# First loads of a batched matmul recut: b's first tile in halves over two queues, one b tile on another queue, an early table load, and a late store in halves

## The chip, the core and the metric

The kernel runs on one core of a Trainium2 chip. The metric is device time in microseconds (us), lower is better. All outputs are right.

## The reference

```python
a = randn(1024, 64, 64)   # fp32
b = randn(1024, 64, 64)   # fp32
out = np.matmul(a, b)     # fp32, 1024 products of 64x64 by 64x64
```

16.78 MB of a and of b are read and 16.78 MB are written.

## The kernel before

a comes in 8 tiles of 128 batches (GpSimd's queue, cast to bf16 in flight), b in 16 tiles of 64 batches (SyncE's and ScalarE's queues, fp32), the output leaves in 16 tiles (GpSimd's queue). Per tile of a: VectorE regroups it, TensorE transposes, ScalarE copies the transposes out of PSUM (the memory in which TensorE's results land in this kernel). Per tile t: VectorE spreads the transposed a into a block-diagonal tile, ScalarE casts b, TensorE multiplies, ScalarE evicts the first half of the product from PSUM and VectorE the second. The parts concerned, with cuts marked:

```python
b_v = b.rearrange("(t g h) (kp u) n -> t (h kp) g (u n)", h=4, g=16, u=2)

def load_b(t):
    b_sb = b_pool.tile([128, 16, 128], fp32, name="b_sb")      # 4 buffers
    queue = nc.scalar if t in (1, 3, 5, 7) else nc.sync
    load = queue.dma_start(out=b_sb[:], in_=b_v[t])
    # ... tiles 0 and 1 wait for the second load of a's first tile
def regroup(s):
    # ...
    nc.vector.tensor_copy(a_bf[:], a_sb[:].rearrange("p h v k -> p v h k"))
def cast(t):
    # ...
    nc.scalar.copy(b_bf[:], b_sb[:])      # last tile: in four, ScalarE and VectorE in turn
def multiply(t):
    # ... products; half 0 evicted by ScalarE, half 1 by VectorE
    held[t] = [lambda: put(0, 8)]         # last tile: four pieces of 2

# main loop, in program order
for t in range(n_t):
    # spread(t+1); cast(t+1); load_b(t+4)
    # on even t: regroup(t//2 + 2), load_a(t//2 + 4)
    # multiply(t); transpose of the a tile ahead; store(t-1)
```

Of the kernel before, what the change touches and what calls it, by code (L numbers as in the profile page):

```python
# [8 lines left out]
fp32 = mybir.dt.float32  # L9
# [4 lines left out]
def kernel(  # L14
# [14 lines left out]
    nc = tc.nc  # L29
# [4 lines left out]
    n_t, n_s = B // 64, B // 128  # L34
# [6 lines left out]
    b_v = b.rearrange("(t g h) (kp u) n -> t (h kp) g (u n)", h=4, g=16, u=2)  # L41
    o_v = out.rearrange("(t gh x) (mo w) n -> t (x mo) gh (w n)", gh=8, x=8, w=4)

    consts = ctx.enter_context(tc.tile_pool(name="consts", bufs=1))
# [12 lines left out]
        consts.tile([128, 2, 16, 2, 4, 16], fp32, name=f"at_bd{i}") for i in range(N_BD)  # L57
    ]
    identity = consts.tile([128, 128], fp32)
    a_tiles, b_tiles, abf_tiles, at_tiles, bbf_tiles = {}, {}, {}, {}, {}  # L60
    held, first_a = {}, []

    def load_a(s):
        a_sb = a_pool.tile([128, 4, 16, 64], bf16, name="a_sb")
        for h in range(4):
            load = nc.gpsimd.dma_start(  # L66
                out=a_sb[:, h, :, :].rearrange("p v k -> p (v k)"), in_=a_v[s, h]
            )
            if s == 0:
                first_a.append(load)  # L70
        a_tiles[s] = a_sb

    def load_b(t):
        b_sb = b_pool.tile([128, 16, 128], fp32, name="b_sb")
        queue = nc.scalar if t in (1, 3, 5, 7) else nc.sync
        load = queue.dma_start(out=b_sb[:], in_=b_v[t])  # L76
        if t < 2:
            tc.add_manual_dep(
                load.ins,
                first_a[1].ins.name,  # L80
                mybir.DependencyInfo(
                    mybir.DependencyClass.Sync, mybir.DependencyReason.DATA
                ),
                reason="first tile of a goes ahead",
            )
        b_tiles[t] = b_sb

    def regroup(s):
        a_sb = a_tiles.pop(s)
        a_bf = work.tile([128, 16, 4, 64], bf16, name="a_bf")  # L90
        nc.vector.tensor_copy(a_bf[:], a_sb[:].rearrange("p h v k -> p v h k"))  # L91
        abf_tiles[s] = a_bf
        at_tiles[s] = work.tile([128, 2, 32, 2, 4, 4], fp32, name="at_sb")

    def transpose(s, j):
        a_cols = abf_tiles[s][:].rearrange("p v h k -> p v (h k)").bitcast(fp32)
        for wl in range(2):
            at_ps = t_psum.tile([128, 4, 128], fp32, name="at_ps")
            for vo in range(4):
                nc.tensor.transpose(  # L100
                    at_ps[:, vo, :], a_cols[:, 4 * vo + 2 * j + wl, :], identity[:]
                )
            nc.scalar.copy(  # L103
                at_tiles[s][:, j, :, wl, :, :],
                at_ps[:].rearrange("p vo (g mp) -> p g mp vo", mp=4),
            )

    def spread(t):
        half = slice(16 * (t % 2), 16 * (t % 2) + 16)
        bd = bd_tiles[t % N_BD]  # L110
        for h in range(4):
            rows = slice(32 * h, 32 * h + 32)
            nc.vector.tensor_copy(  # L113
                bd[rows, :, :, :, h, :].rearrange("p j g wl mo -> p j (g wl) mo"),
                at_tiles[t // 2][rows, :, half, :, :, :].rearrange(
                    "p j g wl mp vo -> p j (g wl) (mp vo)"
                ),
            )

    def cast(t):  # L120
        b_bf = work.tile([128, 16, 128], bf16, name="b_bf")
        b_sb = b_tiles.pop(t)
        if t < n_t - 1:
            nc.scalar.copy(b_bf[:], b_sb[:])  # L124
        else:
            for gq in range(4):
                rows = slice(4 * gq, 4 * gq + 4)
                if gq % 2:
                    nc.vector.tensor_copy(b_bf[:, rows, :], b_sb[:, rows, :])  # L129
                else:  # L130
                    nc.scalar.copy(b_bf[:, rows, :], b_sb[:, rows, :])  # L131
        bbf_tiles[t] = b_bf

    def store(t):
        for piece in held.pop(t):
            piece()

    def multiply(t):
        at_bd = bd_tiles[t % N_BD][:].rearrange("p j g wl h mo -> p j g (wl h mo)")
        at_bd = at_bd.bitcast(bf16).rearrange("p j g (c u) -> p j g c u", u=2)  # L140
        b_bf = bbf_tiles.pop(t)
        last = t == n_t - 1
        o_sb = o_pool.tile([128, 8, 2, 2, 64], fp32, name="o_sb")

        def put(lo, n):
            nc.gpsimd.dma_start(  # L146
                out=o_v[t, :, lo : lo + n, :],
                in_=o_sb[:, lo : lo + n].rearrange("p gh j wl n -> p (gh j wl n)"),
            )

        def evacuate(o_ps, gh, n, copy):

            for par in range(2):
                for wl in range(2):
                    src = o_ps[64 * wl : 64 * wl + 64, :, par, :, :]
                    dst = o_sb[64 * par : 64 * par + 64, gh : gh + n, :, wl, :]
                    copy(dst, src)  # L157

        for half in range(2):
            if not last:  # L160
                o_ps = o_psum.tile([128, 4, 2, 2, 64], fp32, name="o_ps")
            for g8 in range(8):
                if last and g8 % 4 == 0:
                    o_ps = t_psum.tile([128, 2, 2, 2, 64], fp32, name="at_ps")
                g = 8 * half + g8
                gl = (g8 % 4 if last else g8) // 2
                for j in range(2):
                    for u in range(2):
                        nc.tensor.matmul(  # L169
                            o_ps[:, gl, g % 2, j, :],  # L170
                            at_bd[:, j, g, :, u],
                            b_bf[:, g, 64 * u : 64 * u + 64],
                            start=(u == 0),
                            stop=(u == 1),
                        )
                if last and g8 % 4 == 3:
                    copy = nc.scalar.copy if g8 == 3 else nc.vector.tensor_copy
                    evacuate(o_ps, g // 4 * 2, 2, copy)
            if not last:
                copy = nc.vector.tensor_copy if half else nc.scalar.copy  # L180
                evacuate(o_ps, 4 * half, 4, copy)
        if last:
            held[t] = [lambda q=q: put(2 * q, 2) for q in range(4)]
        else:
            held[t] = [lambda: put(0, 8)]

    with tc.manual_schedule():
        load_a(0)
        for t in range(B_AHEAD):
            load_b(t)  # L190
        nc.vector.memset(bd_tiles[0][:], 0.0)  # L191
        make_identity(nc, identity)
        for s in range(1, A_AHEAD):
            load_a(s)
        nc.gpsimd.memset(bd_tiles[1][:], 0.0)  # L195
        regroup(0)
        transpose(0, 0)
        transpose(0, 1)
        spread(0)
        cast(0)  # L200
        regroup(1)
        load_a(A_AHEAD)
        transpose(1, 0)
        for t in range(n_t):
            s, half = t // 2, t % 2
            if t + 1 < n_t:
                spread(t + 1)
                cast(t + 1)
            if t + B_AHEAD < n_t:
                load_b(t + B_AHEAD)  # L210
            if half == 0:
                if s + 2 < n_s:
                    regroup(s + 2)
                if s + 1 + A_AHEAD < n_s:
                    load_a(s + 1 + A_AHEAD)
            multiply(t)
            if half == 0 and s + 1 < n_s:
                transpose(s + 1, 1)
            if half == 1 and s + 2 < n_s:
                transpose(s + 2, 0)  # L220
            if t >= HOLD - 1:
                store(t - HOLD + 1)
        for t in range(n_t - HOLD + 1, n_t):
            store(t)
# [30 lines left out]
```

## Time and profile before

| | before |
|---|---|
| time, median of the first three runs | 136.94 us (136.76 to 137.51) |
| span of the profiled run | 134.8 us |
| VectorE busy | 105.0 us (78%); 90% or more in 26 of the 29 slices from 30.3 to 128.1 us |
| DMA engines busy | 90% or more in the slices from 3.4 to 121.3 us |
| b's tiles 0, 1, 2, 3 landed at | 22.7, 22.9, 33.2, 33.5 us |
| VectorE's spread(2) began at | 32.17 us |
| VectorE's last eviction ended at | 127.9 us |

The prediction shows the lines for the whole run and the tail. More of them count in what follows: the page's row of VectorE's busy tenths in 40 slices of 3.37 us, its count of DMA packets (a packet is one entry of the trace's DMA records), its list of issues for b (columns: tensor, queue, number, KB as the trace encodes the load, us to landing), and the moments of cast(1), of GpSimd's first store and of VectorE's spread(2).

```profile
DVE  5512099069999999997999999997599999999900
DMA packets 17469, 42.12 MB, mean 312 GB/s; under 512 B 1073, under 2 KB 1073, under 8 KB 17457
b_sb<-in_b_dram SPq DMA_DIRECT2D x12, 0.5 KB, 18.3
b_sb<-in_b_dram ACTq DMA_DIRECT2D x4, 0.5 KB, 16.0
```

```profile
25.48 1.91 ACT L124 CAST b_bf<-b_sb 128x2048 bf16<-128x2048 f32 x1
32.73 1.32 POOL L146 DMA_DIRECT2D out_dram<-o_sb  x1 [3.29 <-DVE o_sb L157]
32.17 3.22 DVE L113 COPY at_bd<-at_sb 32x1024 f32<-32x1024 f32 x4
```

There are 1073 packets under 512 bytes and the same 1073 under 2 KB: nothing but semaphore writes and the like lies below 2048 bytes. "0.5 KB" looks odd for a load of 1 MB; it means that the shape is not in the DMA instruction but in a shape register set just ahead of it (the trace has one MOVE_SHAPE per load).

### The profile page before, as it was taken

To read this page: it belongs to the slowest core of one execution; us is meant where nothing else is said; L and a number is where in the kernel's file an instruction comes from. 1 tells how busy PE (TensorE), PEld (TensorE's weight loads), DVE (VectorE), ACT (ScalarE), POOL (GpSimd) and SP (SyncE) were. 2 spreads that over 40 slices of the span, in tenths; PEclk is the share of its full clock that TensorE was granted. 3 is DMA by queue (a packet is one entry of the trace's DMA records).
4 is the path that set the end of the run, shared out by engine and by line. 5 is a ranking of instruction groups with operands and counts; after the bars stand their busy time and mean duration, and the time that the engine had idled before them with its cause. 6 is when DMAs were issued, how large, how long until landed. Compare 5 with 4: busy or idle time off the path is not lost.

```text
span 134.8 us, 2815 instructions
## 1 busy us (share of the span) xinstructions
PE 69.3 (51%) x1152; PEld 65.2 (48%) x1152; DVE 105.0 (78%) x143; ACT 84.5 (63%) x122; POOL 46.6 (35%) x58
## 2 busy tenths in 40 slices
PE   0007305695169709389637861956039735669000
PEld 0007205695069609289637861956039625558000
DVE  5512099069999999997999999997599999999900
ACT  0010902992998995958996896699347996637100
POOL 6949723132413350152322243323021114040820
PEclk9999999999955995955995599599955995555555
DMA  2999999999999999999999999999999999998593
GB/s 19 185 204 261 309 305 301 309 308 279 272 294 311 312 394 346 303 275 361 393 360 273 272 381 396 340 267 288 393 394 396 393 399 395 407 406 350 191 320 136
DMA packets 17469, 42.12 MB, mean 312 GB/s; under 512 B 1073, under 2 KB 1073, under 8 KB 17457
## 3 DMA queue, kind: packets, MB, share of 16 engines
q0 software_dynamic: 9008, 25.17, 66.1%
q1 hardware_dynamic: 6336, 12.58, 26.0%
q10 hardware_dynamic: 2112, 4.19, 8.1%
q8 instruction: 9, 0.15, 0.4%
q14 instruction: 4, 0.02, 0.0%
HBM read 33.55 MB, written 16.78 MB: 373 GB/s over the span
## 4 chain that ended last, share of the span: by engine, by line
DMA 65%; DVE 18%; issue 9%; POOL 3%; POOLq 1%; DVEq 0%
DMA a_sb<-in_a_dram 48%; DMA out_dram<-o_sb 16%; DVE o_sb L157 10%; DVE at_bd L113 8%; POOL out_dram L146 2%; POOL a_sb L66 1%; POOLq L250 1%; DVE a_bf L91 0%; DVEq L91 0%; POOLq L146 0%; DVEq L113 0%; POOLq L239 0%
## 5 line engine op out<-in xcount | busy, mean ns | idle before, releaser
L169 PEld LDWEIGHTS <-at_bd 128*128 128x128 bf16 x1024 | 45.8, 117 | 41.4 <-DVE o_sb L157 30.7
L169 PE MATMUL o_ps<-b_bf,at_bd 128*128 128x64 bf16 x960 | 44.7, 219 | 36.6 <-DVE o_sb L157 28.7
L113 DVE COPY at_bd<-at_sb 32x1024 f32<-32x1024 f32 x64 | 46.4, 725 | 7.9 <-ACT at_sb L103 5.9
L157 DVE COPY o_sb<-o_ps 64x512 f32<-64x512 f32 x60 | 41.3, 688 | 1.8 <-PE o_ps L169 0.8
L157 ACT COPY o_sb<-o_ps 64x512 f32<-64x512 f32 x60 | 34.8, 580 | 9.5 <-DMA out_dram<-o_sb 5.3
L146 POOL DMA_DIRECT2D out_dram<-o_sb x19 | 21.0, 1107 | 46.9 <-DVE o_sb L157 20.1
L124 ACT CAST b_bf<-b_sb 128x2048 bf16<-128x2048 f32 x15 | 28.6, 1905 | 8.7 <-DMA b_sb<-in_b_dram 8.5
L66 POOL DMA_DIRECT2D a_sb<-in_a_dram x32 | 21.5, 681 | 35.2 <-DMA a_sb<-in_a_dram 21.0
L100 PE MATMUL at_ps<-identity,a_bf 128*128 128x128 f32 x128 | 24.4, 357 | 17.3 <-DVE a_bf L91 17.3
L100 PEld LDWEIGHTS at_ps<-identity,a_bf 128*128 128x128 f32 x128 | 20.5, 190 | 17.7 <-issue 17.7
L103 ACT COPY at_sb<-at_ps 128x512 f32<-128x512 f32 x32 | 17.6, 589 | 4.8 <-PE at_ps L100 4.5
L91 DVE COPY a_bf<-a_sb 128x4096 bf16<-128x4096 bf16 x8 | 9.8, 1228 | 11.5 <-DMA a_sb<-in_a_dram 11.3
L76 ACT MOVE_SHAPE b_sb<-in_b_dram x4 | 0.7, 172 | 7.9 <-DMA a_sb<-in_a_dram 7.0
L157 ACT COPY o_sb<-at_ps 64x256 f32<-64x256 f32 x8 | 2.9, 367 | 3.0 <-PE at_ps L169 2.9
L191 DVE MEMSET at_bd<- 128x4096 f32 x1 | 3.5, 3472 | 1.7 <-PEq L239 1.7
L103 ACT ACT_TABLE_LOAD x1 | 1.3, 1283 | 4.8 <-issue 4.8
L169 PE MATMUL at_ps<-b_bf,at_bd 128*128 128x64 bf16 x64 | 3.6, 241 | 1.2 <-DVE at_bd L113 1.2
L195 POOL MEMSET at_bd<- 128x4096 f32 x1 | 3.5, 3530 | 0.0
L157 DVE COPY o_sb<-at_ps 64x256 f32<-64x256 f32 x8 | 3.4, 421 | 0.1
L131 ACT CAST b_bf<-b_sb 128x512 bf16<-128x512 f32 x2 | 1.1, 615 | 1.9 <-DMA b_sb<-in_b_dram 1.9
L129 DVE CAST b_bf<-b_sb 128x512 bf16<-128x512 f32 x2 | 0.8, 424 | 0.0
masks.py:199 POOL TENSOR_SCALAR_AFFINE_SELECT identity<-identity 128x128 f32<-128x128 f32 x1 | 0.3, 287 | 0.1
(5 smaller groups left out, 0.6 us busy)
## 6 DMA issues: line engine op xcount, KB each, us to landing
out_dram<-o_sb POOLq DMA_DIRECT2D x15, 1024.0 KB, 21.8
a_sb<-in_a_dram POOLq DMA_DIRECT2D x32, 256.0 KB, 19.8
out_dram<-o_sb POOLq DMA_DIRECT2D x4, 256.0 KB, 5.3
b_sb<-in_b_dram SPq DMA_DIRECT2D x12, 0.5 KB, 18.3
b_sb<-in_b_dram ACTq DMA_DIRECT2D x4, 0.5 KB, 16.0
```

The source lines that it names most:

```text
L66: load = nc.gpsimd.dma_start(out=a_sb[:, h, :, :].rearrange("p v k -> p (v k)"), in_=a_v[s, h])
L91: nc.vector.tensor_copy(a_bf[:], a_sb[:].rearrange("p h v k -> p v h k"))
L100: nc.tensor.transpose(at_ps[:, vo, :], a_cols[:, 4 * vo + 2 * j + wl, :], identity[:])
L103: nc.scalar.copy(at_tiles[s][:, j, :, wl, :, :], at_ps[:].rearrange("p vo (g mp) -> p g mp vo", mp=4),)
L113: nc.vector.tensor_copy(bd[rows, :, :, :, h, :].rearrange("p j g wl mo -> p j (g wl) mo"), at_tiles[t // 2][rows, :, half, :, :, :].rearrange(
L124: nc.scalar.copy(b_bf[:], b_sb[:])
L146: nc.gpsimd.dma_start(out=o_v[t, :, lo : lo + n, :], in_=o_sb[:, lo : lo + n].rearrange("p gh j wl n -> p (gh j wl n)"),)
L157: copy(dst, src)
L169: nc.tensor.matmul(o_ps[:, gl, g % 2, j, :], at_bd[:, j, g, :, u], b_bf[:, g, 64 * u : 64 * u + 64], start=(u == 0), stop=(u == 1),)
L191: nc.vector.memset(bd_tiles[0][:], 0.0)
L195: nc.gpsimd.memset(bd_tiles[1][:], 0.0)
L250: with _tile.TileContext(nc) as tc:
```

## The change

The intent: shorten the head (b's first tile sooner, transposes sooner, no table load in the way) and the tail (half of tile 14's store sooner).

```diff
+    warm = consts.tile([128, 2], fp32)
...
-        queue = nc.scalar if t in (1, 3, 5, 7) else nc.sync
-        load = queue.dma_start(out=b_sb[:], in_=b_v[t])
+        if t == 0:
+            parts = [(nc.sync, 0, 8), (nc.scalar, 8, 16)]
+        else:
+            parts = [(nc.scalar if t in (1, 5, 7) else nc.sync, 0, 16)]
+        for queue, lo, hi in parts:
+            load = queue.dma_start(out=b_sb[:, lo:hi, :], in_=b_v[t][:, lo:hi, :])
...
-        nc.vector.tensor_copy(a_bf[:], a_sb[:].rearrange("p h v k -> p v h k"))
+        for lo, hi in [(0, 1), (1, 2), (2, 3), (3, 4)] if s == 0 else [(0, 4)]:
+            # ... one copy per quarter
...
-            nc.scalar.copy(b_bf[:], b_sb[:])
+            for lo, hi in [(0, 8), (8, 16)] if t == 0 else [(0, 16)]:
+                nc.scalar.copy(b_bf[:, lo:hi, :], b_sb[:, lo:hi, :])
...
-            held[t] = [lambda: put(0, 8)]
+            whole = t < n_t - 2
+            held[t] = [lambda q=q: put(q, 8 if whole else 4) for q in ([0] if whole else [0, 4])]
...
         load_a(0)
+        nc.vector.memset(warm[:, 0:1], 0.0)
+        nc.scalar.copy(warm[:, 1:2], warm[:, 0:1])
```

More of the change, by code (lines that the diff above doesn't have):

```diff
@@ L74, in load_b @@
         b_sb = b_pool.tile([128, 16, 128], fp32, name="b_sb")
-        queue = nc.scalar if t in (1, 3, 5, 7) else nc.sync
-        load = queue.dma_start(out=b_sb[:], in_=b_v[t])
-        if t < 2:
-            tc.add_manual_dep(
-                load.ins,
-                first_a[1].ins.name,
-                mybir.DependencyInfo(
-                    mybir.DependencyClass.Sync, mybir.DependencyReason.DATA
-                ),
-                reason="first tile of a goes ahead",
-            )
+        if t == 0:
[4 more added lines that the diff above has]
+            load = queue.dma_start(out=b_sb[:, lo:hi, :], in_=b_v[t][:, lo:hi, :])
+            if t < 2:
+                tc.add_manual_dep(
+                    load.ins,
+                    first_a[1].ins.name,
+                    mybir.DependencyInfo(
+                        mybir.DependencyClass.Sync, mybir.DependencyReason.DATA
+                    ),
+                    reason="first tile of a goes ahead",
+                )
         b_tiles[t] = b_sb
@@ L90, in regroup @@
         a_bf = work.tile([128, 16, 4, 64], bf16, name="a_bf")
-        nc.vector.tensor_copy(a_bf[:], a_sb[:].rearrange("p h v k -> p v h k"))
+        for lo, hi in [(0, 1), (1, 2), (2, 3), (3, 4)] if s == 0 else [(0, 4)]:
+            nc.vector.tensor_copy(
+                a_bf[:, :, lo:hi, :],
+                a_sb[:, lo:hi, :, :].rearrange("p h v k -> p v h k"),
+            )
         abf_tiles[s] = a_bf
```

## The prediction

> **What bounds the kernel now.** I read the page's slices first, then stretches of the run, then the packet records of the DMA queues, and only then the engines' timelines. The slices' last two rows:
>
> ```profile
> DMA  2999999999999999999999999999999999998593
> GB/s 19 185 204 261 309 305 301 309 308 279 272 294 311 312 394 346 303 275 361 393 360 273 272 381 396 340 267 288 393 394 396 393 399 395 407 406 350 191 320 136
> ```
>
> The 16 DMA engines are at 90% or more from the second slice to the 37th (3.4 to 124.7 us); no compute engine is. The GB/s row looks uneven, but it counts bytes written, and `a` is read as fp32 and written as bf16. Counting a's bytes as read (twice what is written), I summed the packet records in 1 us bins: 395 to 421 GB/s in nearly every bin from 5 to 43 us, 389 to 405 in 4 us bins up to 124. So the transfers are at one rate, near 400, whatever their mix. All there is to move is 3 x 16.78 MB = 50.3 MB, which is 126 us of a 134.8 us span. What is not saturated is the first 3.4 us and the tail. The stretches of the tail (columns: PE, PEld, DVE, ACT, POOL busy, clock, DMA share, GB/s):
>
> ```profile
> 96.00:123.00 27.00, 16.11 (x281) 15.10 (x282) 26.15 (x37) 17.10 (x27) 5.22 (x4) 0.66 1.03 399
> 124.00:125.00 1.00, 0.45 (x9) 0.28 (x6) 0.96 (x3) 0.97 (x3) 0.04 (x1) 0.50 0.53 201
> 125.00:126.00 1.00, 0.00 (x0) 0.00 (x0) 0.97 (x3) 0.13 (x1) 1.00 (x2) 0.50 0.10 29
> 126.00:127.00 1.00, 0.00 (x0) 0.00 (x0) 0.96 (x3) 0.00 (x0) 1.00 (x2) 0.50 0.59 209
> 127.00:133.00 6.00, 0.00 (x0) 0.00 (x0) 0.91 (x3) 0.00 (x0) 1.69 (x3) 0.50 0.96 317
> ```
>
> The reader sees a hole: 399 GB/s up to 123, then 201, 29, 209, and only 317 afterwards. At 124 us, 2.35 MB of the output were still to go; at 400 GB/s that is 5.9 us, ending at 129.9 and not at 133.0 where the last packet ended. The tail loses 3.1 us. GpSimd and VectorE show why:
>
> ```profile
> 118.22 1.36 POOL L146 DMA_DIRECT2D out_dram<-o_sb  x1 [4.58 <-DVE o_sb L157]
> 124.97 3.00 POOL L146 DMA_DIRECT2D out_dram<-o_sb  x4 [5.38 <-issue]
> 128.23 0.72 POOL L146 DMA_DIRECT2D out_dram<-o_sb  x1 [0.26 <-DVE o_sb L157]
> ...
> 95.80 1.23 DVE L91 COPY a_bf<-a_sb 128x4096 bf16<-128x4096 bf16 x1 [2.33 <-DMA a_sb<-in_a_dram]
> 121.63 2.79 DVE L157 COPY o_sb<-o_ps 64x512 f32<-64x512 f32 x4
> 124.45 3.48 DVE L157 COPY o_sb<-at_ps 64x256 f32<-64x256 f32 x8
> ```
>
> Tile 13's store is issued at 118.22, tile 14's not before VectorE has evicted its second half at 124.42. From 95.8 us, when the last tile of a (a7) has landed at 95.7, VectorE runs without a gap to 127.9. So two clocks set the end: the landing of a7 plus 32 us of VectorE, and the drained DMA queue. The chain of waits agrees: it is DMA until 95.7, VectorE to the end of its evictions, then the last store.
>
> **What the Trainium skill says.** "DMA: Bandwidth & Descriptors", section "Issuing engines are not separate DMA queues": DMAs from ScalarE, SyncE and GpSimd run on the same 16 engines and interleave, and issuing from several saves issue time alone. This trace agrees in total (near 400 GB/s with one, two or three queues active) but the split depends on how many are active. Section "Queues, rings and completion order" says that each DMA engine goes round-robin between rows, by packet. Here: with both b queues active a gets about 195 GB/s and each b queue 104 (12 to 31 us); with SyncE's alone a gets about 255 and b 140 (33 to 37 us). Section "Anatomy of one DMA — SWDGE (gpsimd) path" puts some 2 us of fixed cost on a transfer; here 1.5 us pass from the issue at 124.97 to data at 126.5. "ScalarE: Activation LUTs", "What ACT_TABLE_LOAD costs", gives 1283 ns; the trace's one load took 1283 ns.
>
> **The change part by part.**
>
> *Head, engines.* ScalarE before:
>
> ```profile
> 8.56 4.77 ACTq L76 DMA_DIRECT2D b_sb<-in_b_dram  x1
> 13.37 1.28 ACT L103 ACT_TABLE_LOAD   x1 [4.83 <-issue]
> 14.66 2.05 ACT L103 COPY at_sb<-at_ps 128x512 f32<-128x512 f32 x4
> 22.72 1.90 ACT L124 CAST b_bf<-b_sb 128x2048 bf16<-128x2048 f32 x1 [6.01 <-DMA b_sb<-in_b_dram]
> ```
>
> The early table takes 1.28 us from in front of the copies. The regroup in four pieces (same 1.23 us of work, by estimate 0.3 us each) leaves only the last behind the fourth landing at 9.5, so the transposes start some 0.9 us earlier. The halves of b0 go at 104 GB/s on each of two queues: 0.524 MB take 5.0 us rather than 1.05 MB taking 10, so b0 lands near 17.5 instead of 22.7. The first product starts near 18.5 to 19, some 6 us earlier. But the next step on VectorE, evicting tile 0's second half, stands behind regroup(2) in program order, and that waits for a2's landing at 28.0. A2's bytes were all moved before 27 us, while both b queues were still active, and that stays so. Worth at the end: 0. No gain of the head's engines reaches the queue, which is full anyway.
>
> *Head, later casts.* With b0 on both queues b1 and b2 come behind: 1.57 MB on each at 104.5 GB/s from 11.4 is 26.5, plus 1.3 to land (as b0 had) gives 27.8; before, b1 landed at 22.9 and b2 at 33.2. So cast(1) moves from 25.5 to 27.8, then an eviction (2.4), two copies (1.1) and cast(2) near 33.1, as before (33.27). It costs VectorE perhaps 1 us near 33, hidden under the DMA.
>
> *Fourth b tile to SyncE.* ScalarE's queue now carries 3.67 MB and not 4.19. It is empty from about 26.5 rather than 31.5 until b5 goes out (issue 33.3, data 37.7, unchanged). For 5 us a gets 60 GB/s more: 0.3 MB. The same bytes of b come later. GpSimd's queue runs 0.3 MB ahead from then on; at its 257 GB/s that brings a7 in 1.2 us earlier, 94.5, and with it VectorE's run and all later stores. B's last tile comes 0.33/0.14 = 2.4 us later, 117.5 instead of 115.1. ScalarE casts then at 117.5, VectorE needs its own part near 119.5: it fits, barely.
>
> *Tile 14 in halves.* Its first half was evicted by ScalarE at 119.2. Half a store, 0.524 MB, can be issued near 119.6, right after tile 13's, and be moved in the hole from 123.7. The tail behind it is shorter by 0.524 MB at 330 GB/s (its rate after 126.5): 1.6 us. One issue is added, some 0.7 us on an idle GpSimd.
>
> Sum: 1.6 us from the store, up to 1.2 us from a7; I count the second at 0.7 of its size, 0.8. 136.94 - 2.4 = 134.5.
>
> **The rivals.**
> 1. *Only the tail counts.* A7 lands at 95.7 as before, since b5 or later tiles take the bandwidth back. For it: buffers of b free earlier at the head. Then 136.94 - 1.6 = 135.3.
> 2. *The whole hole closes.* With a7 earlier and the half store in the hole, the queue never runs empty, packets stay at 165 ns (they took 190 ns after 126.5) and the rate stays at 400: last packet 129.9, 3.1 us gained, 133.8. Against it: VectorE's last eviction and the last issue with its 1.5 us cannot come before some 128.2.
> 3. *B becomes the late one.* The final b tiles come 2.4 us later, b15 was already waited for (1.9 us before ScalarE's cast at 115.2), and a late cast(14) or cast(15) stalls products and VectorE. That would eat the 0.8 and more: 135.5 to 137.
> 4. *The head's 6 us reach the end.* Against it: no free DMA time between 4 and 123 us to take them up.
>
> **Range and chances.** The middle of 1 to 3 is 134.5; 133.4 to 136.2 covers the full hole and most of rival 3. The 2% line lies at 134.2, just below my middle: faster 0.40, same 0.57, slower 0.03.
>
> **What would show it.** B0's first cast near 17.5 and first product before 20, yet regroup(2) still near 28. B1 landing near 27.8. A7's regroup at 94 to 95. A store of half size issued near 119 and no stretch under 250 GB/s between 123 and 128. VectorE's last eviction near 126.7. Wrong would be: a7 over 2 us earlier, VectorE idle after a7, or a DMA rate well off 400 in the middle.

## More of the kernel before

On VectorE, regroup(2) stands before the eviction of tile 0, and spread(2) after it. On ScalarE, cast(1) stands before the eviction of tile 0, which stands before the copies that spread(2) needs.

## The result, and the profile after

| | before | after |
|---|---|---|
| time, median of four runs | 136.85 us | 141.65 us (141.43 to 141.96) |
| ratio | | 1.034, 95% interval 1.030 to 1.039 |
| span of the profiled run | 134.8 us | 139.1 us |
| VectorE's spread(2) | 32.17 us | 40.48 us |
| VectorE's last eviction ended | 127.9 us | 134.1 us |
| from there to the end of the span | 6.9 us | 5.0 us |

The change made the kernel slower. A ratio is the mean time of one kernel's fast runs over that of the other's of the same rounds, so it is not quite the ratio of the medians. (The median of before is given with the runs of the same chip each time.)

The page of the changed kernel, the same rows as shown of before:

```profile
GB/s 18 190 194 230 231 234 252 304 307 293 272 296 298 392 326 273 293 393 390 369 273 267 382 398 328 269 297 402 393 392 397 395 396 391 397 270 244 211 319 135
DMA packets 19036, 42.12 MB, mean 303 GB/s; under 512 B 1104, under 2 KB 3152, under 8 KB 19024
b_sb<-in_b_dram SPq DMA_DIRECT2D x1, 512.0 KB, 17.4
b_sb<-in_b_dram ACTq DMA_DIRECT2D x1, 512.0 KB, 18.4
b_sb<-in_b_dram SPq DMA_DIRECT2D x12, 0.5 KB, 21.1
b_sb<-in_b_dram ACTq DMA_DIRECT2D x3, 0.5 KB, 15.9
```

There are now 3152 - 1104 = 2048 packets between 512 bytes and 2 KB. The two halves make exactly 1024 each: 0.524 MB / 1024 = 512 bytes a packet. All other b tiles still move in packets of 2048 bytes. The halves are also listed differently (512.0 KB and not 0.5 KB: an immediate shape, no shape register). In the slices from 10 to 24 us the GB/s row is down (230 to 252, before 261 to 309): it counts written bytes, and more of what moves there is now a.

The packet records say how the engines were shared from 12 to 22 us:

| 12 to 22 us | a | b on SyncE | b on ScalarE |
|---|---|---|---|
| before: packets per us | 46.7 | 51.1 | 51.3 |
| before: GB/s (a as read) | 191 | 105 | 105 |
| after: packets per us | 73.0 | 82.1 | 81.8 |
| after: GB/s (a as read) | 299 | 42 | 42 |

In both kernels the queues move nearly equal numbers of packets, whatever the size of these (the counts show this, not how long one turn is). With packets of a quarter of the size and 1.6 times as many of them, each b queue fell from 105 to 42 GB/s, and a rose. B0's halves landed at 24.1 and 25.1 us, later than the whole tile before (22.7), and b1 and b2, which stand behind them on ScalarE's and SyncE's queues, at 35.2 and 34.8.

The engines after, ScalarE, then GpSimd, then VectorE (columns: start, us, engine, line, operation, tiles, count, and in brackets the idle time before it and what ended it):

```profile
24.13 1.99 ACT L135 CAST b_bf<-b_sb 128x1024 bf16<-128x1024 f32 x2 [9.23 <-DMA b_sb<-in_b_dram]
...
35.19 1.90 ACT L135 CAST b_bf<-b_sb 128x2048 bf16<-128x2048 f32 x1 [8.09 <-DMA b_sb<-in_b_dram]
37.00 1.75 ACT L168 COPY o_sb<-o_ps 64x512 f32<-64x512 f32 x3
...
39.64 0.92 POOL L157 DMA_DIRECT2D out_dram<-o_sb  x1 [14.73 <-ACT o_sb L168]
...
28.67 2.79 DVE L168 COPY o_sb<-o_ps 64x512 f32<-64x512 f32 x4 [3.88 <-PE o_ps L180]
40.48 2.83 DVE L123 COPY at_bd<-at_sb 32x1024 f32<-32x1024 f32 x4 [9.01 <-ACT at_sb L113]
```

Cast(1) waits 8.09 us for b1. Behind it in ScalarE's order stands the eviction of tile 0's first half, so GpSimd waits 14.73 us for its first store, and behind that the copies for spread(2), so VectorE stands idle for 9.01 us. From 40.48 us on VectorE has one gap over 0.15 us, of 0.24 us, up to the end of its last eviction at 134.08: it is the bound for the rest of the run. Before, it had waits of 0.82 and 2.33 us in that stretch, so about 2.9 of the 8.3 us were absorbed; its copies took some 0.7 us more in sum; 8.3 - 2.9 + 0.7 = 6.1 us later at the end. GpSimd's queue also ran dry: GpSimd issued nothing from 24.9 to 39.64 us, since its loads of a stand behind that first store, and the DMA fell to about 290 GB/s (a as read) from 42 to 45 us. The halved store then gave 1.9 us back: from VectorE's last eviction to the end of the span there are 5.0 us here, and 6.9 in the two runs below that are as late and have the store whole (the halving alone, and both halves on one queue).

### The profile page after: what moved, and what is told of

It reads as the page before. It is cut to its first block, busy times and chain, and to the rows that moved or that the text cites. A ratio compares the mean times of both kernels' runs of the same rounds, so it can differ in the third digit from the quotient of the medians.

```text
span 139.1 us, 2821 instructions
## 1 busy us (share of the span) xinstructions
PE 67.8 (49%) x1152; PEld 62.6 (45%) x1152; DVE 106.5 (77%) x147; ACT 84.4 (61%) x123; POOL 46.3 (33%) x59
## 2 busy tenths in 40 slices
DMA packets 19036, 42.12 MB, mean 303 GB/s; under 512 B 1104, under 2 KB 3152, under 8 KB 19024
## 4 chain that ended last, share of the span: by engine, by line
DMA 46%; DVE 28%; issue 14%; POOL 5%; ACT 3%; POOLq 1%; SPq 0%; ACTq 0%
DMA b_sb<-in_b_dram 30%; DMA a_sb<-in_a_dram 16%; DVE at_bd L123 16%; DVE o_sb L168 12%; POOL out_dram L157 4%; ACT b_bf L135 3%; POOL a_sb L67 1%; POOLq L265 1%; DVE a_bf L98 0%; POOLq L157 0%; SPq L81 0%; ACTq L135 0%; POOLq L254 0%
## 5 line engine op out<-in xcount | busy, mean ns | idle before, releaser
L180 PEld LDWEIGHTS <-at_bd 128*128 128x128 bf16 x1024 | 43.9, 114 | 51.9 <-DVE o_sb L168 27.5
L180 PE MATMUL o_ps<-b_bf,at_bd 128*128 128x64 bf16 x960 | 43.1, 216 | 45.9 <-DVE o_sb L168 22.4
L123 DVE COPY at_bd<-at_sb 32x1024 f32<-32x1024 f32 x64 | 47.0, 735 | 15.4 <-ACT at_sb L113 13.5
L157 POOL DMA_DIRECT2D out_dram<-o_sb x20 | 22.2, 1108 | 75.4 <-ACT o_sb L168 27.1
L135 ACT CAST b_bf<-b_sb 128x2048 bf16<-128x2048 f32 (+1 forms) x16 | 28.7, 1798 | 18.0 <-DMA b_sb<-in_b_dram 18.0
L168 ACT COPY o_sb<-o_ps 64x512 f32<-64x512 f32 x60 | 34.8, 579 | 4.3 <-PE o_ps L180 3.8
L110 PE MATMUL at_ps<-identity,a_bf 128*128 128x128 f32 x128 | 23.8, 349 | 15.5 <-DVE a_bf L98 15.5
L110 PEld LDWEIGHTS at_ps<-identity,a_bf 128*128 128x128 f32 x128 | 19.7, 184 | 15.9 <-issue 15.9
L67 POOL DMA_DIRECT2D a_sb<-in_a_dram x32 | 20.1, 638 | 13.1 <-DMA a_sb<-in_a_dram 7.9
L98 DVE COPY a_bf<-a_sb 128x4096 bf16<-128x4096 bf16 (+1 forms) x11 | 10.5, 952 | 5.4 <-DMA a_sb<-in_a_dram 5.2
## 6 DMA issues: line engine op xcount, KB each, us to landing
out_dram<-o_sb POOLq DMA_DIRECT2D x2, 512.0 KB, 5.0
b_sb<-in_b_dram SPq DMA_DIRECT2D x1, 512.0 KB, 17.4
b_sb<-in_b_dram ACTq DMA_DIRECT2D x1, 512.0 KB, 18.4
```

What stands on the lines that cost most here:

```text
L67: load = nc.gpsimd.dma_start(out=a_sb[:, h, :, :].rearrange("p v k -> p (v k)"), in_=a_v[s, h])
L98: nc.vector.tensor_copy(a_bf[:, :, lo:hi, :], a_sb[:, lo:hi, :, :].rearrange("p h v k -> p v h k"),)
L110: nc.tensor.transpose(at_ps[:, vo, :], a_cols[:, 4 * vo + 2 * j + wl, :], identity[:])
L123: nc.vector.tensor_copy(bd[rows, :, :, :, h, :].rearrange("p j g wl mo -> p j (g wl) mo"), at_tiles[t // 2][rows, :, half, :, :, :].rearrange(
L135: nc.scalar.copy(b_bf[:, lo:hi, :], b_sb[:, lo:hi, :])
L157: nc.gpsimd.dma_start(out=o_v[t, :, lo : lo + n, :], in_=o_sb[:, lo : lo + n].rearrange("p gh j wl n -> p (gh j wl n)"),)
```

## The experiments

Theory P: the small packets of the halved load are the cause. Rival Q: moving b's fourth tile to SyncE is. Rival R: halving over two queues is bad whatever the packets, since b1 and b2 stand behind both halves. The tail and the rest of the head were separated from these. Times of before on the same chip were 137.07 us, 137.32 and 137.22.

### B's first tile whole again

The changed kernel, with

```diff
-        if t == 0:
-            parts = [(nc.sync, 0, 8), (nc.scalar, 8, 16)]
-        else:
-            parts = [(nc.scalar if t in (1, 5, 7) else nc.sync, 0, 16)]
+        parts = [(nc.scalar if t in (1, 5, 7) else nc.sync, 0, 16)]
```

> The changed kernel with one thing undone: b's first tile is again one load on SyncE's queue (4th tile still on SyncE, both casts still halved, all else kept). Theory P (the halved load moves in 512-byte packets where a whole tile moves in 2048-byte ones, and since each DMA engine shares by packet, b's queues get 42 GB/s each and not 104): packets of 2048 bytes everywhere, b0 lands near 23, b1 near 23 to 24, cast(1) by 26, VectorE's spread(2) near 32 and not 40; time 134.5 to 135.5 us. Rival Q (it is the 4th b tile's move to SyncE that starves the later tiles): time stays 140 to 142.

Measured: 135.63 us, ratio to before 0.989 (0.986 to 0.991). All b packets 2048 bytes, b0 and b1 landed at 22.1 and 22.3. VectorE of this run:

```profile
31.28 3.09 DVE L120 COPY at_bd<-at_sb 32x1024 f32<-32x1024 f32 x4
...
93.64 1.23 DVE L95 COPY a_bf<-a_sb 128x4096 bf16<-128x4096 bf16 x1
...
119.79 0.76 DVE L137 CAST b_bf<-b_sb 128x512 bf16<-128x512 f32 x2 [1.13 <-DMA b_sb<-in_b_dram]
```

Undoing this one part of the change takes away the whole loss, and Q falls. Without it the rest is 1.4 us faster than before. The last line shows a price of the fourth tile's move: VectorE now waits for b's last tile.

### Halves cut by partitions

```diff
-            parts = [(nc.sync, 0, 8), (nc.scalar, 8, 16)]
+            parts = [(nc.sync, 0, 64), (nc.scalar, 64, 128)]   # of b_sb[lo:hi], all 16 groups
```

> The changed kernel with b's first tile still in halves over both queues, but cut by partitions (64 and 64, each row's 16 groups whole) and not by groups. Theory P: if the packets are 2048 bytes again, b0 lands near 17.5, b1 and b2 near 27.8 (as the prediction reckoned), time 134 to 135.5. Rival R (a halved tile over both queues is bad in itself, since b1 and b2 then wait behind it): with 2048-byte packets the time is still 138 or more. If the packets come out at 512 bytes, both expect about 141.

Measured: 142.05 us, ratio 1.036 (1.033 to 1.039). These halves, too, came in 512-byte packets (1024 on each queue), b0 landed at 24.9 and 25.7, b1 and b2 at 36.4 and 36.3, spread(2) began at 41.75. The hoped-for halves with large packets did not come about, so this run does not tell P from R; it shows that either way of cutting gives small packets and the loss.

### The halving alone

The kernel before, with only the first b tile halved by groups over both queues, b3 on ScalarE.

> The kernel before with only b's first tile halved by groups over both queues; nothing else. Theory P: 512-byte packets, b0 near 25, b1 and b2 near 35, VectorE's spread(2) near 40; slower by the whole loss and without the tail's gain: 142 to 144 us. Rival Q (the 4th tile's move is needed for the loss): 137 to 138.

Measured: 144.30 us, ratio 1.053 (1.049 to 1.056). B0 at 23.7 and 24.8, spread(2) at 40.95. The halving alone is enough for a loss. The time was near the expected, the path was not quite: b1 and b2 landed at 33.7 and 33.5, and ScalarE had one more delay, its issue of b3 took 16.7 us (4.8 before) and kept the table load and the first copies until 25.5. Cast(1) began at 35.62, 1.9 us after b1 had landed, so here it waited for this chain (ScalarE's copies ahead of it waited 3.61 us for transposes) and no longer for b1. In the changed kernel this delay could not arise, since b3 is on SyncE and the table is loaded at 0.74 us.

### Both halves on one queue

```diff
-            parts = [(nc.sync, 0, 8), (nc.scalar, 8, 16)]
+            parts = [(nc.sync, 0, 8), (nc.sync, 8, 16)]        # b1, b3 on ScalarE as before
```

> The kernel before with b's first tile in two halves by groups, both on SyncE's queue, so that no second queue carries it and b1 and b3 stand on ScalarE's queue as before. Theory P (small packets): 512-byte packets, one ring with about 57 packets per us, so 29 GB/s while ScalarE's queue is active and about 41 after it; b0 lands near 40 and not 22.7, VectorE's spread(2) near 47, time 146 to 152 us. Rival R (two queues, b1 and b2 put behind b0, make the loss): order as before, b0 lands by 24, time 136.5 to 138.

Measured, one look: 149.8 us. 2048 packets of 512 bytes on SyncE's queue, first at 10.5 us, b0's halves landed at 27.3 and 38.6, while b1, in large packets on ScalarE's queue, landed at 20.4. From 12 to 22 us SyncE's queue got 63.7 packets per us, ScalarE's 62.2: at 512 and 2048 bytes that is 33 and 127 GB/s, side by side in one run.

```profile
38.69 1.90 ACT L128 CAST b_bf<-b_sb 128x2048 bf16<-128x2048 f32 x1 [22.66 <-DMA b_sb<-in_b_dram]
...
46.74 3.09 DVE L117 COPY at_bd<-at_sb 32x1024 f32<-32x1024 f32 x4
```

This shows that P needs no help from R. No second queue carries b0 and nothing stands in front of b1; the small packets alone make b0 16 us late. R as the only cause falls. What R adds in the changed kernel, where it is b1 behind the slow half that cast(1) waits for, was not measured apart: that would take halves with large packets over two queues, for which the prediction's 27.8 us for b1 is an estimate.

### 12 and 4 groups

```diff
-            parts = [(nc.sync, 0, 8), (nc.scalar, 8, 16)]
+            parts = [(nc.sync, 0, 12), (nc.scalar, 12, 16)]
```

> The changed kernel with b's first tile cut 12 groups to SyncE and 4 to ScalarE. It asks which size of load gives which packets: 1 MB gave 2048 bytes, 0.5 MB gave 512 by either cut. If packets depend on the load's size or its rows per DMA engine, 0.75 MB may come at either and 0.25 MB at 512 or less. Theory P: if the larger part comes in 2048-byte packets, b0's 12 groups land near 20 and the 4 groups near 18, loss mostly gone: 134.5 to 136.5; if in 512-byte packets, its 0.79 MB take 19 us at 42 GB/s, land near 30, and the time is 143 to 146.

Measured, one look: 139.96 us. Both parts came in 512-byte packets (1536 and 512), and the 12 groups landed at 31.1 as P reckoned. The time is below the 143 to 146 expected: the smaller part was through by 17.7, so b1 followed in large packets and was there at 26.4, and cast(1) could follow b0's cast at once; spread(2) began at 39.24. So 0.25, 0.5 and 0.75 MB parts all get small packets, whole 1 MB tiles large ones.

Why is a matter of the built program (this paragraph is read from builds, not from traces). For a whole tile it holds a source of 32 x 16 rows of 512 floats (2048 bytes: the rows of four partitions lie side by side in DRAM) and a destination shape, set by a register, that deals each out to four partitions. For each part it holds rows of 128 floats (512 bytes) for one partition each. Builds with 14 and 2 groups, 15 and 1, and with two separate tiles of 8 groups, which were not run, had 512-byte rows as well. What makes the build choose was not found, so halves with large packets were not tried.

### The halved store alone, the fourth tile alone, and everything but b's loads

The kernel before with only tile 14's store in halves:

> The kernel before with only tile 14's store in halves. Theory: everything up to 118 us as before, the half store issued near 119.6 fills the hole from 123.7, 1.6 us gained: 135.3 us. Rival (the halves cost as much as they gain): 136.9 within 0.3.

Measured: 135.67 us, ratio 0.989 (0.987 to 0.992). The half store went out directly behind tile 13's (two issues from 118.33), and the hole is filled: no 1 us bin between 123 and 128 is under 267 GB/s, where before one had 36:

```profile
118.33 2.16 POOL L146 DMA_DIRECT2D out_dram<-o_sb  x2 [4.58 <-issue]
```

The kernel before with only `t in (1, 5, 7)` for ScalarE's queue:

> The kernel before with only b's fourth tile on SyncE's queue. From the whole-tile run, where a's last tile was regrouped 2.2 us earlier (93.6) and b's last tile landed 4.7 us later (119.8) with the two cancelling: the same here, a7's regroup near 94 and b15 near 119.5, time 136.0 to 137.2, no change over 0.7 us. Rival: it is worth the 1.2 us of the prediction by itself, 135.7.

Measured: 135.83 us, ratio 0.990 (0.988 to 0.993): the rival of the expectation was right. A7's regroup began at 93.35, b15 landed at 119.7, and VectorE ended its evictions near 126.8, 1.1 us earlier than before.

The changed kernel without both changes of b's loads (`t in (1, 3, 5, 7)`, all whole):

> The changed kernel without both changes of b's loads: b0 whole on SyncE, b3 on ScalarE. Left are the early table, the regroup in pieces, the halved casts and the halved store. Theory: the head's engines finish earlier but wait for b0 and a2 as before, so as the halved store alone: 135.67 within 0.4. Rival: the head's parts bring over 0.7 us: under 135.0.

Measured: 135.61 us, ratio 0.989 (0.986 to 0.993), the same as the halved store alone. Early table, regroup in pieces and halved casts bring nothing to the end: ScalarE waited for b0 until 22.07 in this run too.

So the halved store is worth 1.4 us, the fourth tile 1.5 us, and both together (the whole-tile run) 1.4 us. They do not add up. With the fourth tile moved, b15 lands at 119.8. On ScalarE its cast stands before the eviction of tile 14's first half, which therefore began at 121.03 and not at 116.9; all six last stores went out together from 123.68, and the half store filled no hole. Whether this order is what cancels the gain was tested next.

### The last cast behind tile 14's product, and the last pieces on SyncE

The whole-tile run, with `cast(15)` after `multiply(14)` in program order:

> The changed kernel with b's first tile whole on SyncE (as in the whole-tile run, 135.63), and the cast of the last b tile put behind tile 14's product in program order, so that ScalarE evicts tile 14's first half before it waits for b15 (which lands near 119.8), and VectorE evicts the second half before it. Theory (fourth tile's move and halved store gain one thing each, a7 2.2 us earlier and the hole filled, but the late b15 holds back tile 14's eviction and so cancels the second): the half store goes out near 119 and not at 123.7, VectorE ends near 125.8 instead of 126.9, no hole at 124 us; 133.3 to 134.8 us. Rival (the tail is bound by the queue's 330 GB/s after 125 us whatever the order): 135.3 to 135.8.

Measured: 135.53 us, ratio 0.988 (0.985 to 0.991); the expectation missed, and its rival met the time but not the reason, a DMA bound after 125 us. The half store did go out at 120.78 and the DMA stayed at 384 GB/s or more up to 127 us, with no hole. But VectorE ended at 127.7, later than the hoped-for 125.8 and than the 126.9 of the whole-tile run:

```profile
119.85 2.79 DVE L165 COPY o_sb<-o_ps 64x512 f32<-64x512 f32 x4 [1.19 <-PE o_ps L177]
122.67 0.76 DVE L137 CAST b_bf<-b_sb 128x512 bf16<-128x512 f32 x2
124.20 3.49 DVE L165 COPY o_sb<-at_ps 64x256 f32<-64x256 f32 x8 [0.77 <-PE at_ps L177]
```

B14 is late as well (ScalarE waited 2.46 us for it before 112.04), its cast holds back an eviction that frees PSUM for tile 14's product (which began at 116.24, as that eviction ended), and VectorE waits for that product. The last store is issued at 127.98, and the span is 133.6 as in the whole-tile run. A full queue does not help when the last piece is issued no earlier.

The same, with tile 15's four pieces on SyncE's queue:

> The kernel of the cast-after-product run with the four pieces of tile 15's store on SyncE's queue, idle by then, and not GpSimd's. If the last pieces' issue (0.72 us each on GpSimd) or the single queue's rate of 330 GB/s bounds the tail, 0.5 to 1 us less than that run; if the queue's total work does, the same within 0.3; if the smaller packets of SyncE's queue lose to GpSimd's 4096-byte ones, 0.3 to 1 us more.

Measured: 135.22 us, ratio 0.986 (0.983 to 0.989). It is the fastest of all in its median, but its interval overlaps those of the five others from 135.53 to 135.83; whether the last 0.3 us is real, at the edge between two of the expected outcomes, stays open. Each of the six is faster than both kernels of the change, though none by 2%.

## Why the prediction was wrong

**What bounds the kernel now** held for the DMA: one rate near 400 GB/s, a hole at the tail, and the halved store alone filled it. On the other side it read past a row: "no compute engine is" at 90% or more holds over the whole stretch, but not for the part that decided. VectorE's row has a 9 in 26 of the 29 slices from 30.3 to 128.1 us. (The DMA's row, in turn, has its last 9 before the tail in the 36th slice, to 121.3 us, not in the 37th.) So there was little room on VectorE for a late start.

**The step that failed** is in the head: "The halves of b0 go at 104 GB/s on each of two queues: 0.524 MB take 5.0 us rather than 1.05 MB taking 10, so b0 lands near 17.5". They went at 42 GB/s and landed at 24.1 and 25.1. The prediction had the rule (turns by packet, cited from the skill) and the share (104 GB/s), but carried the share over to another load without asking whether its packets are the same size. They were 512 bytes, not 2048.

**Its consequence, the later casts.** "So cast(1) moves from 25.5 to 27.8 [...] It costs VectorE perhaps 1 us near 33, hidden under the DMA." The chain named there was the right one; its input was wrong. Cast(1) began at 35.19, spread(2) 8.3 us later than before, and only some 2.9 us were hidden, for VectorE's gaps behind that point were 0.82 and 2.33 us: VectorE became the bound, and GpSimd's queue ran dry. The run with both halves on one queue shows the same with a later b0: spread(2) at 46.74, 149.8 us.

**"A2's bytes were all moved before 27 us [...] and that stays so."** A2 landed at 23.4, since a had what b lost. It was of no use; the wait that ended last was now b1's. That a wait other than regroup(2) could hold back tile 0's eviction and spread(2) was none of the four rivals: rival 3 had b late, but at the end of the run.

**The fourth tile's move** was right in mechanism and wrong in its sizes, and the sum came out near by luck. In the run of it alone 7.34 MB of a (as read) had been moved at 30 us, against 6.83 before: 0.5 MB ahead and not 0.3. A7 was regrouped 2.4 us earlier (predicted 1.2; "over 2 us earlier" was one of the prediction's signs of being wrong), b15 landed at 119.7 (predicted 117.5), and VectorE's wait of 1.10 us for b15 took a good part of this back. So 1.5 us were gained (predicted "up to 1.2").

**Tile 14 in halves** was predicted at 1.6 us and measured at 1.4 alone. The sum of both, 2.4, was wrong even without the halved load: 1.4 us together. This is rival 3 in outcome: b's last tiles are late and stall what follows their casts. Taking cast(15) out of the way filled the hole but did not bring the gain back, since VectorE then waited behind the late b14.

**The head's engines** were predicted at 0 and measured at 0 (135.61 against 135.67).

**Slips that did not decide.** "The middle of 1 to 3 is 134.5" is the sum's result and not the middle of 135.3, 133.8 and 135.5 to 137, and a range up to 136.2 covers under half of rival 3, not most. The 1.5 us set beside the skill's 2 us is the stretch from an issue to its first data; the skill's figure is for setup and completion, so the two are not one quantity.

## What to carry to other kernels

When DMA queues competed here, a load's share went with its packet size; before cutting a load, compare the packet counts and the issue list of a build or a trace, since a part of a tile may be encoded with smaller rows than the whole. Before calling a delay hidden, look at the later gaps of the engine that it holds up: a mean of 78% busy left VectorE only 3.15 us of them from 32 us on. A load that is "sooner" by its own size can be later in a full queue, and everything issued behind it on that queue is later too, so follow the second and third tile and not only the first. Gains at one end that pass through the same late tile do not add up; measure them together.

## What the Trainium skill lacked or had wrong

- "DMA: Bandwidth & Descriptors", section "Queues, rings and completion order", has the round-robin by packet, and the runs agree (46.7, 51.1 and 51.3 packets per us on three queues; 73.0, 82.1 and 81.8 with small ones). It does not say what follows from it: here bytes were shared nearly in proportion to packet size, 33 GB/s for 512-byte packets beside 127 for 2048-byte ones in one run.
- The same page, section "Rules for kernel authors", advises against two transfers to partition halves since they share the same engines ("Don't bother"). Here it was worse than no gain: such halves moved in 512-byte packets where the whole tile has 2048, and the kernel took 142.05 us against 135.63 with the tile whole.
- The same page mentions reads widened over several rows and shape registers, but no page says that a whole-tile load may be built so while a part of the same tile is not; the sign in the profile is 0.5 KB against 512.0 KB in the list of issues.
- No page has how long an issue can hold its engine behind loads with small packets: ScalarE's issue of b3 took 16.7 us in the run of the halving alone, 4.8 us before.
- The first byte of about 0.6 us for SyncE's and ScalarE's queues in "DMA: Bandwidth & Descriptors", section "Specifications", was not met with the engines busy: b's first load was issued at 7.04 us and its first packet moved at 11.3.
